# The low part of a weight tile: a subtraction on VectorE, or a negated copy on ScalarE and a transfer that adds

## The chip, the core and the metric

The kernel runs on one core of a Trainium2 chip. The time is that of one execution on the device, in microseconds, the median of the runs shown. A core has TensorE for matrix products, VectorE and ScalarE for elementwise work, GpSimd, and 16 DMA engines that move data; SyncE (SP in the profile) and GpSimd (POOL) issue transfers here. All of them run side by side and wait for each other by semaphores. Each engine takes its own instructions strictly in the order of the program.

## What is computed

Two layers of a transformer on 256 latent tokens and 256 context tokens of width 1024, all in float32. Per layer: a gated feed-forward, a mixer, another gated feed-forward, each with a norm that is modulated by a conditioning vector. The mixer of layer 0 is neighbourhood attention beside a long convolution, that of layer 1 is retention. In the last layer only the latents go on after the mixer.

```python
def swiglu(h, w_in, w_out):
    a, b = jnp.split(h @ w_in, 2, axis=-1)
    return (jax.nn.silu(a) * b) @ w_out
...
        mod_l = (jax.nn.silu(c) @ w_mod[i] + b_mod[i]).reshape(b, N_MOD, 1, D_MODEL)
        x_lat = x_lat + 0.5 * mod_l[:, 2] * swiglu(modulate(x_lat, norm_gain[i, 0], mod_l[:, 0], mod_l[:, 1]),
                                                 ffn_a_in[i], ffn_a_out[i])
...
            o_l, o_c = na_hyena_mixer(h_l, h_c, even_in[e], even_out[e], ...)
            o_l, o_c = retention_mixer(h_l, h_c, ret_in[o], ret_out[o], ...)
```

## The kernel before, in words

Tokens lie along the free axis of a tile and features along its 128 partitions; lat and ctx share one tile of 512 columns. Each float32 product is made of three products in the faster type `fp32r`: a number is split into a high part, its rounding to fp32r, and a low part, what is left. `mm3` (L207 to L210) adds high times high, high weight times low activation, and low weight times high activation; the last of the three is the one that reads the low part of the weight, `wlo`.

Weights come as 336 tiles of 128 x 1024 (512 KB) or, for the feed-forward's second matrix, 128 x 1408 (704 KB), listed in `worder` in the order of use. A tile goes through these steps, each in four buffers:

- `w_dma` (L132): SP issues the load of a tile into one of four raw buffers, `raw`.
- `w_split` (L142): ScalarE copies `raw` into `whi`, which rounds it; VectorE subtracts `whi` from `raw` into `wlo`. Then `w_dma` loads the tile that is to take the same raw buffer.
- `w_get` (L172): hands a tile to TensorE. Ahead of it, it splits up to three more tiles. So the split of the tile after the next two stands in the program right before TensorE's work on the present one, and its `whi` and `wlo` buffers are those of the tile TensorE has just left.

Two rarer ways to split are `w_halves` (the first four tiles) and `w_paged` (seven tiles at the norms, into other buffers).

The modulation vectors are made beside this on VectorE: `mod_step` (L226) takes one 512 KB tile `wm` of the modulation weights, multiplies it with the conditioning vector and sums it (the reductions `junk`, L237), and `m_dma` loads another. Two such steps go with each pair of tiles in most feed-forwards, so SP's order there is raw, raw, wm, wm. There are two buffers for `wm`.

A feed-forward has two halves. In each, 11 pairs of tiles (`pi`) give a gate and a value, which ScalarE and VectorE turn into the activation `sg` and its parts `ghi` and `glo`; then 8 tiles of 704 KB (`po`) add to the residual. On both streams a weight tile feeds 512 columns; in the last feed-forward and from the retention's output on only 256. The order of the work is that of the program (`manual_schedule`); nothing is reordered.

Of the kernel before, what the change touches and what calls it, by code (L numbers as in the profile page):

```python
# [30 lines left out]
# columns of the packed per-partition constants  # L31
# [18 lines left out]
def _mod_tiles():  # L50
    """(layer, index, feature block) of the modulation VectorE makes, in order."""
    return [(l, i, b) for l, i in [(0, j) for j in range(2, 9)] + [(1, j) for j in range(9)] for b in range(KB)]


def body(ctx, tc, I, out):
# [38 lines left out]
    # ---------------------------------------------------------------- constants  # L94
# [11 lines left out]
    # ---------------------------------------------------------------- weights  # L106
# [35 lines left out]
    def w_split():  # L142
        i = wpos["split"]
        if i >= len(worder):
            return
        while wpos["dma"] <= i:
            w_dma()
        n = worder[i][1]
        t = raws.pop(i)
        hi = whl.tile([P, WSLOT], F32R, tag="hi", name="whi")  # L150
        lo = whl.tile([P, WSLOT], F32R, tag="lo", name="wlo")
        act(hi[:, :n], t[:, :n], AF.Copy)
        V.tensor_tensor(out=lo[:, :n], in0=t[:, :n], in1=f(hi[:, :n]), op=ALU.subtract)  # L153
        hls[i] = (hi, lo)
        wpos["split"] += 1
        if not hold[0]:
            w_dma()

    def w_halves():
        """The next tile's split in two steps; nothing is loaded in its place."""  # L160
# [22 lines left out]
    def w_paged():  # L183
        """The next tile, split into pages: for where whl's buffers are all in use."""
# [27 lines left out]
    # ---------------------------------------------------------------- modulation  # L212
# [37 lines left out]
    # ---------------------------------------------------------------- residual and norms  # L250
# [8 lines left out]
    def sumsq(s, m, late=None):  # L259
        """Adds block m's squares; the addition itself is left to the caller where a list is given."""  # L260
# [16 lines left out]
    def rsqrt_steps(y, src, scale, n):  # L277
        """y (SBUF) = (src*scale + eps)^-1/2, src in PSUM; one VectorE operation between yields."""
# [25 lines left out]
    def norm_h(s, k, l, n, dst):  # L304
        """dst: (hi, lo) APs of block k, stream s. Returns what is left to do once hi is there."""
# [25 lines left out]
    # H: list of KB (hi, lo), each [P, 512] = lat | ctx  # L331
# [15 lines left out]
    class Norm:  # L347
        """Norm n of layer l, whose sums of squares are complete per stream in turn."""
# [29 lines left out]
    # ---------------------------------------------------------------- generic matrix products  # L378
    def out_gemm(acts, nk, tiles_per_m, l, n, lat_only, norm, late_acts=None):
        """X += gate * (W^T acts); acts: list of (hi, lo) [P, 512] or [P, 256]."""  # L380
# [85 lines left out]
    def first_group(norm, mid=None):  # L466
        """The first 4 feature tiles after a norm; the latents go first, the context's norm runs beside."""
# [39 lines left out]
    def scaled(norm, k):  # L507
        """Block k of the latents times the gain, not yet normed, for the products that run ahead of the norm.
        Two more columns hold the shift."""
# [14 lines left out]
    def first_group_lat(norm):  # L524
        """The first 4 feature tiles of a norm of the latents alone. They run ahead of the norm, whose factor
        of each row and whose shift's product the evacuation adds."""
# [43 lines left out]
    # ---------------------------------------------------------------- SwiGLU  # L570
# [52 lines left out]
    # ---------------------------------------------------------------- start  # L623
    FILT = {}

    def dft_load(j):
        """Table j of the transforms in two parts."""
# [5 lines left out]
    def parted(a, j):  # L633
        """a[j] becomes its two parts."""
# [79 lines left out]
    def decay_scalars():  # L714
        """Decay exponents: log_sigmoid of the logits."""
# [20 lines left out]
    def start():  # L736
# [78 lines left out]
        def normed(s, m):  # L815
            """Blocks 2m and 2m+1 of stream s, normed."""
# [93 lines left out]
    # ---------------------------------------------------------------- layer 0 mixer  # L910
    def mixer0(norm_in, norm_out):
# [62 lines left out]
        # attention  # L974
# [9 lines left out]
        def qk_split(b):  # L984
            """Queries and keys of heads 2b and 2b + 1 in two parts each."""
# [89 lines left out]
        def attend(i):  # L1075
            """One step of the attention: head i's scores, head i-1's transposes, head i-2's values."""
# [17 lines left out]
        # queries and keys  # L1094
# [19 lines left out]
        # values  # L1114
# [17 lines left out]
        # hyena projections, with the attention beside them  # L1132
# [93 lines left out]
    # ---------------------------------------------------------------- layer 1 mixer  # L1226
    def mixer1(norm_in, norm_out):
# [74 lines left out]
        def qk_parts(h):  # L1302
            """Queries and keys of head h in two parts each."""
            parted(kT[h], 0)
            parted(kT[h], 1)
            parted(qT, h)
# [119 lines left out]
def _layout(inp):  # L1426
# [4 lines left out]
    def featT(x):  # (256, 1024) -> (4, 128, 2*256)  # L1431
# [5 lines left out]
    def pcol(v):  # (..., n*128) -> (128, ...*n)  # L1437
# [29 lines left out]
    # first shift and scale: chunks of 2 feature blocks of each, per block of 128 inputs  # L1467
# [3 lines left out]
    def feat_tiles(w, n):  # (n*128? K, C) -> (C/128, 128, K/128*128)  # L1471
# [13 lines left out]
    def tok_tiles(w):  # (1024, C) -> chunks of 256 columns, halves of K: (C/256*2, 128, 4*256)  # L1485
# [22 lines left out]
    ph = 2 * np.pi * np.outer(np.arange(L), np.arange(L) + 0.5) / 512  # [t, k]  # L1508
# [5 lines left out]
    # relative position bias laid out per (query, key); keys outside the window hold a constant  # L1514
# [36 lines left out]
```

## Time and profile before

| | |
|---|---|
| Time, median of 3 runs | 1912.69 us (1911.32 to 1914.88) |
| Profiled execution, first to last instruction | 1918.3 us |
| TensorE busy | 1894.8 us, 99% |
| VectorE busy | 1210.1 us, 63% |
| of it subtractions for `wlo` (L153), 325 | 421.8 us |
| ScalarE busy | 701.5 us, 37% |
| GpSimd busy | 65.6 us, 3% |
| moved by SP's transfers | 273.76 MB |
| moved by GpSimd's transfers | 2.10 MB |

For the profiled execution the page gives its span and no other time; the span is 5.6 us over the median of the runs.

How to read it: an engine's busy time is the time its instructions ran, not the time it was needed. TensorE's matmuls overlap and their ends are modelled, so its pace is better read from the count in a stretch than from one matmul's length. A line can be that of a helper: all ScalarE copies stand at L89, so the tile's name tells them apart. "A <- B" in the list of waits says that A was held up by B, with total, times and longest. A stretch (a:b) is a piece of the span in microseconds; its row has the busy time and the count of each engine, then the granted TensorE clock, the mean busy share of the 16 DMA engines and the GB/s that they moved.

### The profile page before, as it was taken

The numbers are of one execution on the slowest core, as the hardware profiler recorded it, in microseconds if no ns is written. First come the engines' busy times: TensorE is split into PE (matmuls) and PEld (weight loads), VectorE is DVE, ScalarE is ACT, GpSimd is POOL, SyncE is SP. The second block draws the span as 40 slices with busy tenths as digits, with TensorE's granted clock in tenths as the row PEclk, the third lists the DMA queues.
The fourth block names the chain that finished last, engine by engine and source line by source line (L and its number), as shares of the span: only waits on it lengthen the run. The fifth ranks groups of instructions, "written<-read, shape, count | busy, mean of one in ns | idle before, by whom it ended". The sixth has DMA issues, their size and how long they took to land.

```text
span 1918.3 us, 26355 instructions
## 1 busy us (share of the span) xinstructions
PE 1894.8 (99%) x10646; PEld 1627.5 (85%) x10646; DVE 1210.1 (63%) x1870; ACT 701.5 (37%) x1085; POOL 65.6 (3%) x73
## 2 busy tenths in 40 slices
PE   8999999999999999999999999999999999999999
PEld 5788888798877798878887988888889999999999
DVE  5577677777676776676766655433346755567554
ACT  4332122245554352222222422122233544465442
POOL 1010000002001200000000000000000200000000
PEclk9999999999999999999999999999999999999999
DMA  9355445532323235554555256423323432355653
GB/s 355 117 175 197 150 165 183 200 95 82 99 66 92 77 108 166 174 197 144 185 193 169 85 190 209 142 88 94 116 82 99 133 100 88 100 178 184 197 181 129
DMA packets 77899, 277.52 MB, mean 145 GB/s; under 512 B 8657, under 2 KB 9681, under 8 KB 77650
## 3 DMA queue, kind: packets, MB, share of 16 engines
q1 hardware_dynamic: 76626, 273.76, 43.2%
q0 software_dynamic: 1152, 2.10, 0.4%
q8 instruction: 83, 1.36, 0.3%
q14 instruction: 38, 0.31, 0.0%
HBM read 274.77 MB, written 1.05 MB: 144 GB/s over the span
## 4 chain that ended last, share of the span: by engine, by line
PE 87%; DMA 5%; DVE 5%; issue 1%; ACT 1%; SPq 0%; POOL 0%; DVEq 0%; POOLq 0%; ACTq 0%
PE pi L208 13%; PE pi L209 13%; PE pi L210 13%; PE po L209 9%; PE po L208 9%; PE po L210 9%; DMA wm<-in_wmt_dram 5%; DVE wlo L153 2%; PE fg L208 2%; PE fg L210 2%; PE fg L209 2%; PE pv L1297 2%; PE pv L1296 2%; PE pv L1295 2%; DVE junk L237 1%
## 5 line engine op out<-in xcount | busy, mean ns | idle before, releaser
L208 PE MATMUL pi<-hhi,whi 128*128 128x512 f32 (+1 forms) x1488 | 545.9, 367 | 0.0
L210 PE MATMUL pi<-hhi,wlo 128*128 128x512 f32 (+1 forms) x1488 | 545.2, 366 | 0.0
L209 PE MATMUL pi<-hlo,whi 128*128 128x512 f32 (+1 forms) x1488 | 545.2, 366 | 0.0
L153 DVE TENSOR_TENSOR wlo<-raw,whi 128x1024 fp32r<-128x1024 f32 (+1 forms) x325 | 421.8, 1314 | 165.5 <-ACT whi L89 164.9
L89 ACT ACTIVATE whi<-raw 128x1024 fp32r<-128x1024 f32 (+1 forms) x329 | 363.9, 1115 | 394.0 <-PE po L209 161.5
L237 DVE CUSTOM_DVE_ANT_0 junk<-wm,scb,cst 128x1024 bf16<-128x1024 f32 x224 | 291.1, 1299 | 97.0 <-DMA wm<-in_wmt_dram 93.2
L208 PEld LDWEIGHTS pi<-hhi,whi 128*128 128x128 f32 x1488 | 279.8, 188 | 52.2 <-issue 1.1
L210 PEld LDWEIGHTS pi<-hhi,wlo 128*128 128x128 f32 x1488 | 279.6, 188 | 49.5
L209 PEld LDWEIGHTS pi<-hlo,whi 128*128 128x128 f32 x1488 | 279.6, 188 | 49.2
L208 PE MATMUL po<-ghi,whi 128*128 128x512 f32 (+1 forms) x770 | 271.1, 352 | 6.9 <-ACT ghi L89 6.9
L209 PE MATMUL po<-glo,whi 128*128 128x512 f32 (+1 forms) x770 | 270.2, 351 | 0.2 <-DVE glo L181 0.2
L210 PE MATMUL po<-ghi,wlo 128*128 128x512 f32 (+1 forms) x770 | 270.1, 351 | 0.0
L89 ACT ACTIVATE ghi<-sg 128x512 fp32r<-128x512 f32 (+1 forms) x88 | 50.9, 579 | 396.7 <-DVE sg L580 393.5
L208 PEld LDWEIGHTS po<-ghi,whi 128*128 128x128 f32 x770 | 145.7, 189 | 29.1 <-ACT ghi L89 8.2
L209 PEld LDWEIGHTS po<-glo,whi 128*128 128x128 f32 x770 | 145.8, 189 | 22.4 <-DVE glo L181 1.5
L210 PEld LDWEIGHTS po<-ghi,wlo 128*128 128x128 f32 x770 | 145.7, 189 | 20.4
L391 DVE SCALAR_TENSOR_TENSOR x<-po,gate,x 128x256 f32<-128x256 f32 x136 | 61.3, 480 | 126.2 <-PE po L210 125.9
L580 DVE TENSOR_TENSOR sg<-sg,pi 128x512 f32<-128x512 f32 (+1 forms) x79 | 49.1, 622 | 100.3 <-PE pi L210 99.1
L181 DVE TENSOR_TENSOR glo<-sg,ghi 128x512 fp32r<-128x512 f32 (+1 forms) x88 | 55.1, 626 | 56.9 <-ACT ghi L89 56.9
L89 ACT ACTIVATE sq<-x 128x256 f32<-128x256 f32 (+1 forms) x71 | 30.1, 439 | 120.3 <-DVE x L391 120.2
L1297 PE MATMUL pv<-whi,hlo 128*128 128x256 f32 x256 | 72.1, 282 | 0.0
L1295 PE MATMUL pv<-whi,hhi 128*128 128x256 f32 x256 | 72.1, 282 | 0.0
(331 smaller groups left out, 2438.7 us busy)
## 6 DMA issues: line engine op xcount, KB each, us to landing
raw<-in_ffi_dram SPq DMA_DIRECT2D x176, 512.0 KB, 3.7
wm<-in_wmt_dram SPq DMA_DIRECT2D x128, 512.0 KB, 4.5
raw<-in_ffo_dram SPq DMA_DIRECT2D x64, 704.0 KB, 4.8
raw<-in_rt_dram SPq DMA_DIRECT2D x64, 512.0 KB, 3.7
raw<-in_ev_dram SPq DMA_DIRECT2D x32, 512.0 KB, 3.6
wm<-in_wm_dram SPq DMA_DIRECT2D x32, 256.0 KB, 5.7
x<-in_xt_dram SPq DMA_DIRECT2D x8, 256.0 KB, 5.4
bias<-in_rpb_dram SPq DMA_DIRECT2D x8, 256.0 KB, 4.2
```

Source lines behind the costliest of these rows:

```text
L89: S.activation(out=out, in_=in_, func=func, **k)
L153: V.tensor_tensor(out=lo[:, :n], in0=t[:, :n], in1=f(hi[:, :n]), op=ALU.subtract)
L181: V.tensor_tensor(out=lo, in0=src, in1=f(hi), op=ALU.subtract)
L208: T.matmul(o, lhsT=w[0][:, c0:c1], rhs=x[0][:, x0:x1], start=start, stop=False)
L209: T.matmul(o, lhsT=w[0][:, c0:c1], rhs=x[1][:, x0:x1], start=False, stop=False)
L210: T.matmul(o, lhsT=w[1][:, c0:c1], rhs=x[0][:, x0:x1], start=False, stop=stop)
L237: V.tensor_tensor_reduce(out=junk, in0=t, in1=scb[:, s, :], scale=1.0, scalar=bcol, op0=ALU.mult, op1=ALU.add, accum_out=MOD[l][:, idx, b, ...
L391: V.scalar_tensor_tensor(out=xs(s, m), in0=p[:, c0:c0 + L], scalar=gate[:, m, s:s + 1], in1=xs(s, m), op0=ALU.mult, op1=ALU.add)
L580: V.tensor_tensor(out=sg, in0=sg, in1=pb[:, :w], op=ALU.mult)
L1295: T.matmul(po[tb], lhsT=H[k][0][:, hs_], rhs=w[0][:, ws_], start=k == 0, stop=False)
L1296: T.matmul(po[tb], lhsT=H[k][0][:, hs_], rhs=w[1][:, ws_], start=False, stop=False)
L1297: T.matmul(po[tb], lhsT=H[k][1][:, hs_], rhs=w[0][:, ws_], start=False, stop=k == KB - 1)
```

## The change

In `w_split` the low part is made in two steps. ScalarE writes minus the high part into `wlo`. Then a transfer that GpSimd issues reads `raw` and adds it onto what stands in `wlo`, so that `wlo` holds raw minus high as before. `w_halves`, `w_paged` and `split_to` keep VectorE's subtraction. The rest of the difference is comments taken out.

```diff
@@ w_split
         act(hi[:, :n], t[:, :n], AF.Copy)
-        V.tensor_tensor(out=lo[:, :n], in0=t[:, :n], in1=f(hi[:, :n]), op=ALU.subtract)
+        act(lo[:, :n], f(hi[:, :n]), AF.Copy, scale=-1.0)
+        G.dma_start(out=lo[:, :n], in_=t[:, :n], accum_op=ALU.add)
         hls[i] = (hi, lo)
```

Three places show how the instructions move. In all of them a name ends in a buffer number, "waits" lists what the instruction's engine waits for, DMAHW is a transfer of SP and DMASW one of GpSimd, and the line numbers of the changed kernel are one higher. The first is ScalarE in the last feed-forward, before and with the change, two pairs of tiles:

```order
L89 ACTIVATE whi_15914<-raw_15780 128x1024 [waits DMAHW1_49,PE_49,Activation_49]
L89 ACTIVATE whi_15945<-raw_15811 128x1024 [waits DMAHW2_49,PE_49,Activation_49]
L89 ACTIVATE sg_15976<-pi_15920 128x256 [waits PE_49]
L89 ACTIVATE ghi_15979<-sg_15976 128x256 [waits DVE_49]
L89 ACTIVATE whi_15983<-raw_15849 128x1024 [waits DMAHW3_49,PE_49,Activation_49]
```

```order
L89 ACTIVATE whi_15942<-raw_15805 128x1024 [waits DMAHW1_49,PE_49]
L89 ACTIVATE wlo_15943<-whi_15942 128x1024 [waits DMASW4_49,PE_49,Activation_49]
L89 ACTIVATE whi_15974<-raw_15837 128x1024 [waits DMAHW2_49,PE_49]
L89 ACTIVATE wlo_15975<-whi_15974 128x1024 [waits DMASW5_49,PE_49,Activation_49]
L89 ACTIVATE sg_16006<-pi_15949 128x256
L89 ACTIVATE ghi_16009<-sg_16006 128x256 [waits DVE_49]
```

Between a pair's activations there are four copies of a whole tile where there were two, and the added ones wait for TensorE to leave the buffer and for the transfer that added into it four tiles earlier.

The second is SP, whose raw loads in the same stage stood as the first fence shows and stand as the second does:

```order
L138 DMA raw_14502<-in_ffi_dram 128x1024 [waits DMAHW1_49,DVE_49]
L138 DMA raw_14527<-in_ffi_dram 128x1024 [waits DMAHW2_49,DVE_49]
L138 DMA raw_14540<-in_ffi_dram 128x1024 [waits DMAHW3_49,DVE_49]
L138 DMA raw_14553<-in_ffi_dram 128x1024 [waits DMAHW4_49,DVE_49]
L138 DMA raw_14566<-in_ffi_dram 128x1024 [waits DMAHW5_49,DVE_49]
```

```order
L138 DMA raw_14775<-in_ffi_dram 128x1024 [waits DMAHW1_49,DMASW0_49,Activation_49]
L138 DMA raw_14801<-in_ffi_dram 128x1024 [waits DMAHW2_49,DMASW1_49,Activation_49]
L138 DMA raw_14815<-in_ffi_dram 128x1024 [waits DMAHW3_49,DMASW2_49,Activation_49]
L138 DMA raw_14829<-in_ffi_dram 128x1024 [waits DMAHW4_49,DMASW3_49,Activation_49]
L138 DMA raw_14843<-in_ffi_dram 128x1024 [waits DMAHW5_49,DMASW4_49,Activation_49]
```

The order is the same; the raw buffer is now released by GpSimd's transfer and no longer by VectorE.

The third is GpSimd with the change, in the same stage; before, its queue is empty there:

```order
L154 DMA wlo_15604<-raw_15440 128x1024 [waits DMAHW0_49,DMASW3_49,Activation_49]
L154 DMA wlo_15646<-raw_15482 128x1024 [waits DMAHW1_49,DMASW4_49,Activation_49]
L154 DMA wlo_15688<-raw_15524 128x1024 [waits DMAHW2_49,DMASW5_49,Activation_49]
L154 DMA wlo_15730<-raw_15566 128x1024 [waits DMAHW3_49,DMASW6_49,Activation_49]
L154 DMA wlo_15762<-raw_15608 128x1024 [waits DMAHW4_49,DMASW7_49,Activation_49]
```

Each waits for ScalarE's negated copy.

## The prediction

> **What bounds the kernel now.** I read the page's busy shares first, then who made TensorE wait, then the chain of waits, then the transfers.
>
> ```profile
> span 1918.3 us, 26355 instructions
> PE 1894.8 (99%) x10646; PEld 1627.5 (85%) x10646; DVE 1210.1 (63%) x1870; ACT 701.5 (37%) x1085; POOL 65.6 (3%) x73
> q1 hardware_dynamic: 76626, 273.76, 43.2%
> q0 software_dynamic: 1152, 2.10, 0.4%
> ```
>
> TensorE is busy for 1894.8 of 1918.3 us. Nothing that makes another engine lighter can win more than the 23.5 us that are left. The transfers hold the 16 DMA engines for 43.2% of the span, 828.7 us for 273.76 MB, so a megabyte costs 3.03 us and a 512 KB tile (0.524 MB) 1.59 us of all 16 engines. That is the resource with the second largest claim, once it is read stage by stage.
>
> ```profile
> PE po L208 <- ACT ghi L89: 6.9, 3, 3.0
> PE pf L647 <- DMA cst<-in_cst_dram: 4.4, 1, 4.4
> SPq L138 <- DVE wlo L153: 1381.5, 305, 24.0
> ```
>
> Of TensorE's idle time 4.4 us is the wait for the first constants. The largest item that VectorE can be blamed for is 6.9 us: three times an output product waits for an activation tile `ghi` whose input comes late from VectorE. The last row shows what the load queue lives on: SP stands before a raw load until VectorE's subtraction has released the raw buffer, 305 times. The chain shows what makes VectorE late at those three places:
>
> ```profile
> 273.33 2.29 DVE wlo L153 x2
> 276.02 6.48 DMA wm<-in_wmt_dram
> 282.63 1.28 DVE junk L237
> 284.13 1.04 issue
> 285.25 2.28 DVE wlo L153 x2
> ```
>
> From one pair of subtractions to the next is 11.9 us: the subtractions release the raw buffers, SP issues the raw loads and then the modulation load behind them, that lands 6.48 us later, and its reductions keep VectorE from the next pair. TensorE needs less for the same pair of tiles: 48 matmuls at 52.00/225 us (the stretch 208 to 260 below), 11.1 us. VectorE falls behind by 0.8 us a pair until TensorE notices. This is a real cost of the subtraction, and it is small.
>
> **The change, part by part.** Removed: 325 subtractions on VectorE. Added: as many copies with a factor of -1 on ScalarE, and as many transfers issued by GpSimd that read the raw tile and the negated tile and write the sum.
>
> ```profile
> L153 DVE TENSOR_TENSOR wlo<-raw,whi 128x1024 fp32r<-128x1024 f32 x261 | 318.7, 1238 | 138.7 <-ACT whi L89 138.2
> L153 DVE TENSOR_TENSOR wlo<-raw,whi 128x1408 fp32r<-128x1408 f32 x64 | 103.4, 1623 | 26.7 <-ACT whi L89 26.7
> L89 ACT ACTIVATE whi<-raw 128x1024 fp32r<-128x1024 f32 x265 | 276.5, 1053 | 290.3 <-issue 122.9 <-PE po L209 89.2 <-PE pi L209 30.2
> L89 ACT ACTIVATE whi<-raw 128x1408 fp32r<-128x1408 f32 x64 | 87.6, 1374 | 103.8 <-PE po L209 72.3 <-issue 28.2 <-ACT whi L89 3.3
> ```
>
> VectorE loses 318.7 + 103.4 = 422 us and is worth at most the 6.9 us above, because elsewhere TensorE does not wait for it. I count 0 for the gain: the modulation loop keeps its transfer and gets a longer wait ahead of it (below), so the lag need not go.
>
> ScalarE gains 261 x 1.053 + 64 x 1.374 = 363 us, by the row of the same copy: 701.5 becomes 1064 us, 55%. Over the whole span TensorE covers this. In the last stage it nearly fills ScalarE:
>
> ```profile
> 1829.69 1.06 ACT L89 ACTIVATE whi<-raw 128x1024 fp32r<-128x1024 f32 x1 [0.87 <-ACT whi L89]
> 1830.65 0.37 ACT L89 ACTIVATE sg<-pi 128x256 f32<-128x256 f32 x1
> 1833.47 0.42 ACT L89 ACTIVATE ghi<-sg 128x256 fp32r<-128x256 f32 x1 [2.46 <-DVE sg L580]
> 1833.80 1.04 ACT L89 ACTIVATE whi<-raw 128x1024 fp32r<-128x1024 f32 x1
> ```
>
> A pair of tiles there has four copies of 1.05 us now, and 0.37 + 0.42 us: 5.0 us, against 2 x 24 matmuls at 175.00/1476 us (stretch 1690 to 1865 below), 5.7 us. ScalarE still fits, so 0. Without that cover it would cost the pair what goes over 5.7 us.
>
> The transfers are the heavy part. 261 tiles of 0.524 MB and 64 of 0.721 MB are 183 MB, two thirds of what the kernel moves now. No row shows a transfer that adds, so its price per byte is bounded in units of a load's 1.59 us per 512 KB. From below: its bytes need not come from the chip's main memory, so a little under one load, 0.7, can't be excluded. From above: two reads and one write, one after the other, each at a load's full price, make 3. A load reads once and writes once; this reads twice and writes once. If reading sets the pace it costs 2, if the total does 1.5. I take 2 (3.18 us a tile), since the only software-issued transfers in the trace, 0.4% of the span or 7.7 us for 2.10 MB, at 3.65 us a megabyte, lean dear rather than cheap.
>
> The Trainium skill's page "Collectives: The Full Stack" (section on the bandwidth ceiling) says that a reducing transfer is slower not by its addition but because it reads two sources through one read ring; it states a ratio of 1.93 to a plain copy. By that figure my price would be 3.07 us instead of 3.18 us, an estimate; no run here shows it yet.
>
> Where does it fit? Per stretch of the trace I add to the DMA share that is there the new demand: the subtraction's busy time in the stretch over 1.226 us (its median for a 512 KB tile) times 3.18 us, a factor of 2.6. What goes over the stretch's length is time. The first row has that median; then come the stretches, with DMA share and GB/s at the end of a row, and below them the subtraction alone in the same ones:
>
> ```profile
> L153 DVE TENSOR_TENSOR wlo<-raw,whi x325: 1205/1226/2310, 58.3 to 1900.7; 128x1024 fp32r<-128x1024 f32 x131, 128x1408 fp32r<-128x1408 f32 x32
> 156.00:208.00 52.00, 52.00 (x226) 41.98 (x225) 40.16 (x57) 11.47 (x11) 0.00 (x0) 1.00 0.57 191
> 208.00:260.00 52.00, 52.00 (x225) 42.03 (x224) 33.46 (x50) 11.59 (x14) 0.00 (x0) 1.00 0.43 145
> 260.00:362.00 102.00, 100.29 (x433) 80.87 (x431) 74.26 (x101) 25.94 (x33) 0.00 (x0) 1.00 0.53 181
> 783.00:1063.00 280.00, 275.38 (x1216) 223.22 (x1215) 192.97 (x275) 72.40 (x89) 0.00 (x0) 0.99 0.53 177
> 1170.00:1215.00 45.00, 45.00 (x196) 36.34 (x195) 26.22 (x34) 11.89 (x12) 0.00 (x0) 1.00 0.62 210
> 1690.00:1865.00 175.00, 174.88 (x1476) 174.82 (x1477) 114.90 (x165) 89.97 (x140) 0.00 (x0) 1.00 0.59 190
> 1865.00:1918.00 53.00, 49.99 (x422) 49.78 (x421) 24.90 (x28) 16.37 (x19) 0.00 (x0) 1.00 0.43 139
> ...
> 156.00:208.00 52.00, 14.02 (x9) 1.00 0.57 191
> 260.00:362.00 102.00, 22.41 (x18) 1.00 0.53 181
> 783.00:1063.00 280.00, 60.18 (x45) 0.99 0.53 177
> 1170.00:1215.00 45.00, 10.86 (x7) 1.00 0.62 210
> 1690.00:1865.00 175.00, 73.51 (x60) 1.00 0.59 190
> 1865.00:1918.00 53.00, 17.77 (x12) 1.00 0.43 139
> ```
>
> The stretch 1690 to 1865 is the last feed-forward on the latents alone, where a weight tile feeds half as many columns: 0.59 x 175 = 103 us of transfers, plus 73.51 x 2.6 = 191 us, make 294 us in 175: 119 over. The others, in order: 14.0, 10.2, 24.5, 11.1 and, for the last, 15.9. Sum 194.6 us. The stretches left out have room at this price; the longest, 1215 to 1690, keeps 44 us of it.
>
> Three waits are added. GpSimd's issue waits for ScalarE's second copy; behind it in GpSimd's queue stand only the other transfers and some 12 small subtractions, which wait for ScalarE anyway. SP's raw load waits for the adding transfer instead of the subtraction; behind it stand the modulation loads, and behind these the reductions. TensorE's third product waits for the transfer. Between stages these waits are covered by three tiles of matmuls; at the very start they are not:
>
> ```profile
> 57.24 2.01 ACT L89 ACTIVATE whi<-raw 128x1024 fp32r<-128x1024 f32 x2 [2.86 <-PE fg L209]
> 58.33 2.36 DVE L153 TENSOR_TENSOR wlo<-raw,whi 128x1024 fp32r<-128x1024 f32 x2 [3.48 <-ACT whi L89]
> 25.02 0.54 POOL L630 DMA_DIRECT2D dfthi<-in_dft_dram  x1
> dfthi<-in_dft_dram POOLq DMA_DIRECT2D x4, 256.0 KB, 5.3
> raw<-in_ffi_dram SPq DMA_DIRECT2D x176, 512.0 KB, 3.7
> ```
>
> The first split of the steady loop ends at 59.6 and TensorE takes it at once. Now the copy ends at 59.4, the issue takes 0.54, and landing takes 3.7 us by a raw load's row to about 6 by GpSimd's own loads: 4 to 7 us late, once; I take 6.
>
> A raw buffer's round in the narrow stage is then a load of 3.7 us, two copies of 1.06, an issue of 0.54, the addition with about 6, and SP: 12.4 us for four tiles, 3.1 us each. That is over TensorE's 2.85 us a tile but under the 4.8 us that load and addition hold the DMA engines, 1.59 + 3.18, so the engines decide and not the round.
>
> Sum: 194.6 + 6 = 201 us on the profiled span of 1918.3. That span is 5.6 us above the median of the runs shown, 1912.69, and I take the difference as it is: **2113 us**.
>
> **The rivals.**
>
> Cheap addition: the price is about one load. The same table at 1.59 us leaves only the last feed-forward over, by 23.6 us; with the start, 1942 us. For it: half of the reading is on the chip. Against it: twice the bytes read.
>
> Dear addition: three loads or more. The table gives 600 us at three; 2519 us. Then nearly all stretches are bound by transfers. For it: the additions are done row by row in engines whose arithmetic no row shows. Against it: nothing in the trace.
>
> The other side: VectorE's loop of 11.9 us against 11.1 was the lag, it goes with the subtraction, and the transfers fit. This gives back the 6.9 us and costs 4.2 us at the start with the quick landing, so 1910 us, or 1906 if the first copies come early enough. It decides only where an addition costs under 0.85 of a load, since in the narrow stage two plain loads, 3.18 us, already exceed a tile's 2.85 us. The Trainium skill's page "DMA: Bandwidth & Descriptors" (section on the anatomy of one DMA) would put it here: its fit of 2.0 us plus bytes over 436 GB/s makes 3.2 us for 512 KB, 1.2 us of it moving, an estimate of 0.76 of a load. But that fit is for copies.
>
> **How the numbers follow.** Price 1.5 to 2.4 loads (2003 to 2245 us by the same table): 0.56, the forecast. About one load, 1925 to 2003: 0.16. Dearer than 2.4: 0.19. No loss: 0.09, of which 0.04 is faster by over 0.2% and 0.05 within it (0.2% is about what a measurement of this kernel can tell from no change). Slower is 0.91. The forecast's own range is 2003 to 2245; 1940 to 2480 (a price of 2.9) leaves out the no-loss cases and half of the dear ones, together 2 in 10.
>
> **What would show it.** Right: the DMA share rises to nine tenths and more in the last three slices; TensorE waits for GpSimd's transfers at the third product there and hardly elsewhere but in the modulation stretches; the software queue of the page shows 183 MB more at about 6 us a megabyte, some 1110 us of its share. Wrong: if the share stays under 0.9 while TensorE waits, latency and not throughput is the limit; if slices in the middle, 362 to 783 and 1215 to 1690, stretch, the price is above 2.4.

## The result, and the profile after

The changed kernel takes 2119.18 us, the median of 4 runs (2108.07 to 2127.23), against 1913.79 us (1911.32 to 1916.76, 4 runs) for the kernel before: 1.1077 times as long, 95% interval 1.1038 to 1.1116. The forecast was 2113 us with a range of 1940 to 2480. The total is right to 6 us. The parts of the sum are not, and the experiments below show in the main why they made up for each other.

First the page of the changed kernel: span, busy times, and the two queues (packets, MB, share of the 16 DMA engines).

```profile
span 2125.4 us, 27260 instructions
PE 1959.3 (92%) x10646; PEld 1669.6 (79%) x10646; DVE 798.4 (38%) x1545; ACT 1061.4 (50%) x1410; POOL 338.3 (16%) x398
q0 software_dynamic: 47952, 185.09, 46.4%
q1 hardware_dynamic: 76626, 273.76, 37.5%
```

VectorE lost 412 us of work, ScalarE gained 360, and the span grew by 207.1 us. GpSimd's queue holds the 16 engines for 46.4% of 2125.4 us, 986 us for 185.09 MB: 5.33 us a megabyte, 2.80 us for a 512 KB tile. A load costs 37.5%, 2.91 us a megabyte, 1.53 us a tile. An adding transfer is thus worth 1.83 of this kernel's loads, or 1.76 of the loads before.

Next the list of waits, the load queue's and TensorE's (total, times, longest):

```profile
SPq L138 <- DMA wlo<-raw: 1680.5, 318, 27.4
...
PE pi L211 <- DMA wlo<-raw: 66.0, 43, 4.4
...
PE po L211 <- DMA wlo<-raw: 42.7, 22, 6.1
...
PE fg L211 <- DMA wlo<-raw: 21.6, 6, 5.3
...
PE po L209 <- ACT ghi L89: 17.7, 5, 7.1
```

L211 is the third product, the one that reads the low part. TensorE waits there for GpSimd's transfer, as the prediction said, but the row of `fg` is at norms, where it said that three tiles of matmuls cover the wait. Then the transfers' landing (KB each, median us from issue to landing):

```profile
wlo<-raw POOLq DMA_DIRECT2D x261, 512.0 KB, 6.5
raw<-in_ffi_dram SPq DMA_DIRECT2D x176, 512.0 KB, 5.6
wm<-in_wmt_dram SPq DMA_DIRECT2D x128, 512.0 KB, 7.7
```

A raw load of the feed-forward took 3.7 us before. The stretches of the changed kernel that hold the same matmuls as those of the prediction (busy time of each engine, then the granted clock, DMA share, GB/s):

```profile
162.30:218.30 56.00, 53.98 (x226) 42.95 (x225) 25.91 (x44) 21.13 (x18) 6.42 (x8) 0.97 1.01 272
...
381.50:819.40 437.90, 420.38 (x2286) 352.77 (x2287) 231.15 (x469) 237.31 (x413) 73.26 (x75) 0.97 0.65 167
819.40:1126.90 307.50, 283.34 (x1215) 227.79 (x1214) 141.80 (x240) 126.80 (x138) 38.75 (x45) 0.97 0.93 247
...
1292.50:1785.50 493.00, 478.37 (x2962) 427.78 (x2960) 145.27 (x302) 270.27 (x341) 87.91 (x97) 1.00 0.83 198
1785.50:2044.60 259.10, 202.65 (x1476) 194.31 (x1477) 42.43 (x105) 150.54 (x194) 47.73 (x56) 0.92 0.99 245
2044.60:2125.00 80.40, 58.44 (x422) 56.81 (x420) 7.26 (x16) 32.45 (x32) 11.19 (x13) 0.89 0.86 211
```

With every stretch cut at the same matmuls in both traces, the 207.1 us lie here. The last two columns belong to an experiment below, the change with the modulation loads issued one step earlier.

| stretch of before | long before | forecast | after | measured | reordered loads | over before |
|---|---|---|---|---|---|---|
| 0–54 | 54.0 | 0 | 53.9 | −0.1 | 51.8 | −2.2 |
| 54–156 | 102.2 | +6 | 108.3 | +6.1 | 108.8 | +6.6 |
| 156–208 | 52.0 | +14.0 | 56.0 | +4.0 | 52.0 | 0.0 |
| 208–260 | 51.8 | 0 | 51.8 | 0.0 | 51.8 | 0.0 |
| 260–362 | 102.8 | +10.2 | 111.4 | +8.6 | 100.1 | −2.7 |
| 362–783 | 420.3 | 0 | 437.9 | +17.6 | 429.0 | +8.7 |
| 783–1063 | 279.9 | +24.5 | 307.5 | +27.6 | 272.7 | −7.2 |
| 1063–1170 | 107.1 | 0 | 115.2 | +8.1 | 112.7 | +5.6 |
| 1170–1215 | 45.1 | +11.1 | 50.4 | +5.3 | 45.1 | 0.0 |
| 1215–1690 | 474.9 | 0 | 493.1 | +18.2 | 494.8 | +19.9 |
| 1690–1865 | 174.9 | +118.9 | 259.1 | +84.2 | 254.1 | +79.2 |
| 1865 to the last matmul | 50.2 | +15.9 | 77.7 | +27.5 | 70.3 | +20.1 |

So there are three groups: the last feed-forward (the last two rows) with +111.7 us where 134.8 were forecast; the four stretches with modulation that the table charged, +45.5 for 59.8; and all the others, +49.9, where only the 6 us of the start were (they stand at 59.6 in the prediction, so in 54–156). These are the numbers of one trace each: in that of a variant below, with the change ahead of tile 260 alone, the same four stretches are 60.8 us longer and not 45.5. What is called the last feed-forward here, as in the prediction, begins with the rest of the retention's output, which also feeds 256 columns; that ends at 1726.7 in the kernel before.

### The profile page after: what moved, and what is told of

It is laid out like the page before. It is cut to its first block, busy times and chain, and to the rows that moved or that the text cites. A ratio compares the mean times of both kernels' runs of the same rounds, so it can differ in the third digit from the quotient of the medians.

```text
span 2125.4 us, 27260 instructions
## 1 busy us (share of the span) xinstructions
PE 1959.3 (92%) x10646; PEld 1669.6 (79%) x10646; DVE 798.4 (38%) x1545; ACT 1061.4 (50%) x1410; POOL 338.3 (16%) x398
## 3 DMA queue, kind: packets, MB, share of 16 engines
q0 software_dynamic: 47952, 185.09, 46.4%
q1 hardware_dynamic: 76626, 273.76, 37.5%
## 4 chain that ended last, share of the span: by engine, by line
PE 36%; issue 32%; DMA 22%; DVE 3%; POOL 3%; ACT 3%; POOLq 0%; SPq 0%; ACTq 0%; DVEq 0%
DMA wlo<-raw 11%; PE pi L209 5%; PE pi L211 5%; PE pi L210 5%; DMA raw<-in_ffo_dram 3%; DMA raw<-in_ffi_dram 3%; DMA wm<-in_wmt_dram 3%; POOL wlo L154 3%; PE po L211 2%; PE po L209 2%; PE po L210 2%; ACT whi L89 1%; DMA raw<-in_rt_dram 1%; PE pv L1297 1%; PE pv L1298 1%
## 5 line engine op out<-in xcount | busy, mean ns | idle before, releaser
L211 PE MATMUL pi<-hhi,wlo 128*128 128x512 f32 (+1 forms) x1488 | 558.4, 375 | 66.1 <-DMA wlo<-raw 66.0
L209 PE MATMUL pi<-hhi,whi 128*128 128x512 f32 (+1 forms) x1488 | 554.3, 373 | 0.0
L210 PE MATMUL pi<-hlo,whi 128*128 128x512 f32 (+1 forms) x1488 | 552.8, 372 | 0.0
L154 POOL DMA_DIRECT2D wlo<-raw x325 | 280.5, 863 | 1686.3 <-ACT wlo L89 1412.0
L211 PEld LDWEIGHTS pi<-hhi,wlo 128*128 128x128 f32 x1488 | 286.6, 193 | 128.3 <-DMA wlo<-raw 78.4
L89 ACT ACTIVATE wlo<-whi 128x1024 fp32r<-128x1024 f32 (+1 forms) x325 | 365.0, 1123 | 10.3
L210 PEld LDWEIGHTS pi<-hlo,whi 128*128 128x128 f32 x1488 | 286.8, 193 | 49.9
L211 PE MATMUL po<-ghi,wlo 128*128 128x512 f32 (+1 forms) x770 | 277.2, 360 | 24.9 <-DMA wlo<-raw 24.8
L211 PEld LDWEIGHTS po<-ghi,wlo 128*128 128x128 f32 x770 | 151.1, 196 | 48.2 <-DMA wlo<-raw 27.9
L211 PE MATMUL fg<-hhi,wlo 128*128 128x256 f32 (+1 forms) x200 | 63.0, 315 | 15.8 <-DMA wlo<-raw 15.8
L182 DVE TENSOR_TENSOR glo<-sg,ghi 128x512 fp32r<-128x512 f32 (+1 forms) x88 | 55.1, 626 | 56.9 <-ACT ghi L89 56.9
L1297 PE MATMUL pv<-wlo,hhi 128*128 128x256 f32 x256 | 71.9, 281 | 1.3 <-DMA wlo<-raw 1.3
```

Of the source, the lines that this page charges most:

```text
L89: S.activation(out=out, in_=in_, func=func, **k)
L154: G.dma_start(out=lo[:, :n], in_=t[:, :n], accum_op=ALU.add)
L182: V.tensor_tensor(out=lo, in0=src, in1=f(hi), op=ALU.subtract)
L209: T.matmul(o, lhsT=w[0][:, c0:c1], rhs=x[0][:, x0:x1], start=start, stop=False)
L210: T.matmul(o, lhsT=w[0][:, c0:c1], rhs=x[1][:, x0:x1], start=False, stop=False)
L211: T.matmul(o, lhsT=w[1][:, c0:c1], rhs=x[0][:, x0:x1], start=False, stop=stop)
```

## The experiments

The theory was that of the prediction: transfers bind the last feed-forward and the modulation stretches by throughput. The rivals are ScalarE's longer queue, the landing of the low part in front of the third product, and rounds of waits between SP, GpSimd, VectorE and ScalarE. Each time stands beside the kernel before on the same chip (medians 1913.89 to 1914.33 us).

**The price of adding: a copying transfer.** The same transfer, without the addition.

```diff
-        G.dma_start(out=lo[:, :n], in_=t[:, :n], accum_op=ALU.add)
+        G.dma_start(out=lo[:, :n], in_=t[:, :n])
```

> As the changed kernel, but GpSimd's transfer copies the raw tile over the low part instead of adding it, so the low part holds the raw tile and the result is not the reference's. Same number, size, issue and waits; one read less per byte. Theory (engine time of the two reads sets the loss): the price falls from 2.80 us per 512 KB tile (46.4% of 2125.4 us for 185.09 MB) to about a load's 1.5 to 1.6, so by the table of the prediction some 25 us in the narrow stage and some 20 to 40 us at stage edges: 1950 to 1980 us. Rival (the length of the chain of a tile, not the engines' time): landing falls only from 6.5 to about 5 us and most of the loss stays, over 2040 us.

Measured: 1970.24 us, ratio 1.0285 (1.0256 to 1.0314). Its software queue:

```profile
q0 software_dynamic: 47952, 185.09, 26.3%
```

The span there is 1959.5 us, so the same 185.09 MB take 515 us of the engines, 2.78 us a megabyte. Adding costs 5.33 / 2.78 = 1.92 times as much, and the 512 KB tile lands after 4.2 us instead of 6.5. Adding instead of copying is worth 149 us of the kernel; no run here tells the second read from the addition itself. The Trainium skill's page "Collectives: The Full Stack" (section on the bandwidth ceiling) states 1.93 for a reducing transfer against a copying one, measured between cores; the runs here agree, for a transfer inside one core's own memory.

**ScalarE alone.** The negated copy stays; VectorE adds in place of the transfer.

```diff
         act(lo[:, :n], f(hi[:, :n]), AF.Copy, scale=-1.0)
-        G.dma_start(out=lo[:, :n], in_=t[:, :n], accum_op=ALU.add)
+        V.tensor_tensor(out=lo[:, :n], in0=t[:, :n], in1=f(lo[:, :n]), op=ALU.add)
```

> ScalarE writes the negated high part as in the changed kernel, but VectorE adds the raw tile onto it; no adding transfer. Theory (the transfers cost the time): 1914 us as before, at most 10 us more for the longer chain of a tile. Rival (ScalarE's 325 added copies, 363 us, hold up its queue): most of the 205 us stays, 2050 us or more.

Measured: 1956.35 us, ratio 1.0225 (1.0204 to 1.0246), 42 us over the kernel before: a miss. The loss is in the last feed-forward, whose two stretches went from 174.9 to 202.4 and from 50.2 to 56.9 us. ScalarE's timeline there (start, duration, instruction, what it waited for):

```profile
1886.21 0.42 ACT L89 ACTIVATE ghi<-sg 128x256 fp32r<-128x256 f32 x1 [1.36 <-DVE sg L581]
1886.54 1.04 ACT L89 ACTIVATE whi<-raw 128x1024 fp32r<-128x1024 f32 x1
1887.61 1.06 ACT L89 ACTIVATE wlo<-whi 128x1024 fp32r<-128x1024 f32 x1
1888.58 1.05 ACT L89 ACTIVATE whi<-raw 128x1024 fp32r<-128x1024 f32 x1
1889.66 1.06 ACT L89 ACTIVATE wlo<-whi 128x1024 fp32r<-128x1024 f32 x1
1890.62 0.37 ACT L89 ACTIVATE sg<-pi 128x256 f32<-128x256 f32 x1
1892.34 0.42 ACT L89 ACTIVATE ghi<-sg 128x256 fp32r<-128x256 f32 x1 [1.35 <-DVE sg L581]
```

From one `ghi` to the next are 6.13 us; TensorE's pair takes 5.7. The 5.0 us of work that the prediction counted are there, but ScalarE takes its instructions in order and idles 1.36 us between `sg` and `ghi`, until VectorE has multiplied. Counting the work left out the gap. But 0.43 us in each of 22 pairs is under 10 of the 34.2 us that the two stretches lost; the rest was not taken apart. In this variant VectorE's addition also stands behind the copy, so the 42 us are an upper bound for the copies.

**The transfer alone, as a copy.** Neither negated copy nor addition.

```diff
-        act(lo[:, :n], f(hi[:, :n]), AF.Copy, scale=-1.0)
-        G.dma_start(out=lo[:, :n], in_=t[:, :n], accum_op=ALU.add)
+        G.dma_start(out=lo[:, :n], in_=t[:, :n])
```

> GpSimd's transfer copies the raw tile into the low part's place and ScalarE writes no negated part, so its two copies per pair in the narrow stage are as before the change; the low part holds the whole raw tile instead of the remainder. The variant with a copying transfer and the negated copy took 1970, the variant with the negated copy and no transfer 1956. If what is left there of the loss is ScalarE's queue in the narrow stage, this one loses it: 1915 to 1935 us, and the stretch of 174.9 us is at most 185. If it is the transfer itself (two loads' worth per tile, 103 + 88 = 191 us of the DMA engines in 174.9), it stays at 1950 to 1970 us.

Measured: 1924.60 us, ratio 1.0058 (1.0036 to 1.0080). The two stretches are 189.3 and 54.3 us long. The total is what the theory of ScalarE's queue expected, the first stretch is 4 us above its limit. So of the copying variant's loss in the last feed-forward (+37.1 us) half needs ScalarE's copies; alone they gave +34.2, the copying transfer alone +18.5. They overlap, they do not add.

**The adding transfer alone, from tile 262 on.** That is the retention's output from its third tile and the last feed-forward. Nobody reads the sum, and of 704 KB tiles only 512 KB are moved. Two waits are added all the same: ScalarE's next copy into the same buffer of the high part waits until the transfer has read it, and GpSimd's transfer waits for the one before the last, which adds into the same half of the table.

```diff
         V.tensor_tensor(out=lo[:, :n], in0=t[:, :n], in1=f(hi[:, :n]), op=ALU.subtract)
+        if i >= 262:
+            c = i % 2 * D
+            G.dma_start(out=scb.rearrange("p a b -> p (a b)")[:, c:c + D], in_=f(hi[:, :D]), accum_op=ALU.add)
```

> VectorE's subtraction stays in every tile. From the last feed-forward on (tiles 262 to 335) GpSimd issues besides, per tile, an adding transfer of 512 KB whose source is the high part and whose destination is a table that nobody reads any more; no engine waits for its result but the next writer of that high part. So ScalarE has no added copy, SP and TensorE no added wait: only the load on the 16 DMA engines is added. Theory (the DMA engines' throughput makes the narrow stage long): at 2.80 us per added 512 KB, as the changed kernel's software queue shows, the stretch of 174.9 us needs 103 + 60 x 2.80 = 271 us, so +96, and the tail 23 + 12 x 2.80 = 57 for 50, so +6: about 2015 us, 1985 to 2030, with a DMA share of 0.9 and more there. Rival (ScalarE's longer queue and the landing of the low part make it long, the engines only look busy): under +40, at most 1955 us.

Measured: 1987.54 us, ratio 1.0386 (1.0361 to 1.0412). Its stretches with the matmuls of the last feed-forward, then the two added waits in the whole run:

```profile
1680.90:1910.90 230.00, 198.82 (x1476) 188.16 (x1477) 109.77 (x159) 88.55 (x134) 46.88 (x54) 0.95 1.03 264
1910.90:1981.60 70.70, 57.63 (x422) 55.70 (x420) 27.32 (x32) 20.61 (x24) 13.93 (x16) 0.88 0.98 240
```

```profile
POOL scb L156 <- DMA scb<-whi: 186.9, 56, 6.2
...
ACT whi L89 <- DMA scb<-whi: 104.8, 48, 4.1
```

The DMA share is 1.03 and 0.98 and the stretches are 55.1 and 20.4 us longer, without a copy more on ScalarE. That is 75.5 of the change's 111.7 us, and the 16 tiles of 704 KB there would add 0.197 MB each, 16 x 0.197 x 5.33 = 17 us of the engines: an estimate of 92 us. So the transfers by themselves, with no wait of TensorE for their sum, carry most of the loss. That this is throughput and not the two added waits is argued from their own time: in the first stretch the software queue has 65.5% of the 230 us for 28.56 MB and the load queue 37.2%, together 236 us of transfers where TensorE needs 174.9. The price is no effect of the crowd: 5.27 us a megabyte here, and 5.41 in 1292.5–1785.5 of the changed kernel, at a share of 0.83 (50.8% of 493 us for 46.29 MB). No run has the transfers without any added wait, and what the remaining 20 us are, queue or landing, no run here separates.

**The two halves of the change.** Once only from tile 260 on (the retention's output and the last feed-forward), once only ahead of it, with `i < 260` in the condition.

```diff
+        if i >= 260:
             act(lo[:, :n], f(hi[:, :n]), AF.Copy, scale=-1.0)
             G.dma_start(out=lo[:, :n], in_=t[:, :n], accum_op=ALU.add)
+        else:
+            V.tensor_tensor(out=lo[:, :n], in0=t[:, :n], in1=f(hi[:, :n]), op=ALU.subtract)
```

> The change for the last 76 tiles alone (the retention's output product and the last feed-forward, which feed 256 columns); all tiles before them are split by VectorE. Theory (the narrow stage loses by itself, 84 and 27 us in the two stretches of the changed trace): 2015 to 2035 us. Rival (the narrow stage was late from what came before it): under 1980 us.

> The change only in tiles 0 to 259, that is everywhere but in the last feed-forward. The mirror of the kernel that had it only there and took 2021, 107 us over before. If the two halves of the loss add up, this one takes 2119 - 107 = 2012 us (2000 to 2020). My table of stretches gave 14.0 + 10.2 + 24.5 + 11.1 + 6 at the start = 66 us for this part at two loads, and 15 to 25 at the 1.75 loads that the changed kernel's queue showed: 1930 to 1940 us if only throughput and the start count there. So about 2012 says that some 75 us come from something the table leaves out.

Measured: 2021.18 us, ratio 1.0573 (1.0535 to 1.0611), and 2018.64 us, ratio 1.0549 (1.0523 to 1.0575). The halves add: 107 + 104 = 211 us, against 205. The wide half is thus as dear as the narrow one, and the table gave it 66 us.

**The order of the modulation loads.** The changed kernel, with `m_dma` one tile ahead, so that a modulation load no longer stands behind the raw loads of its own pair.

```diff
-            while mpos["dma"] <= i:
+            while mpos["dma"] <= min(i + 1, len(mlist) - 1):
```

> The changed kernel with the modulation tiles' loads one step earlier in SP's order, as in the variant that took 1904. If a good part of the change's loss in the wide stages is SP's order (a modulation load behind raw loads that wait for an adding transfer, and VectorE late behind that), it takes 2070 to 2095 us. If the low part's landing before the third product makes that loss, the order of SP's loads does little: 2100 to 2125 us.

Measured: 2050.59 us, ratio 1.0718 (1.0694 to 1.0742), 69 us less than the change, beyond what either theory gave. Four of its stretches, with the same matmuls as 156–208, 260–362, 783–1063 and 1170–1215 of before:

```profile
160.60:212.60 52.00, 52.00 (x225) 42.07 (x224) 26.83 (x46) 21.33 (x18) 6.45 (x8) 1.00 1.04 295
264.40:364.50 100.10, 100.10 (x433) 81.14 (x432) 54.44 (x84) 48.46 (x53) 15.49 (x18) 1.00 1.03 287
793.60:1066.20 272.60, 272.60 (x1215) 222.47 (x1214) 136.97 (x228) 123.50 (x132) 37.03 (x43) 1.00 1.00 275
1179.00:1224.00 45.00, 45.00 (x195) 36.43 (x194) 13.19 (x22) 21.23 (x19) 6.02 (x7) 1.00 1.03 305
```

In all four TensorE is busy without a gap, at the full clock, while the same tiles are added by the same transfers. The DMA share is 1.00 to 1.04, higher than in the change itself. So throughput did not cost time in these stretches: the share alone does not tell a stage that is bound by transfers from one that they just fill. What cost time is a round of waits. The timeline of the changed kernel without TensorE, inside 783–1063 of before:

```profile
856.03 5.26 SPq L138 DMA_DIRECT2D raw<-in_ffo_dram  x2
...
861.40 2.72 SPq L223 DMA_DIRECT2D wm<-in_wmt_dram  x2
...
873.10 1.28 DVE L238 CUSTOM_DVE_ANT_0 junk<-wm,scb,cst 128x1024 bf16<-128x1024 f32 x1 [13.29 <-DMA wm<-in_wmt_dram]
...
875.64 0.68 DVE L581 TENSOR_TENSOR sg<-sg,pi 128x512 f32<-128x512 f32 x1
...
876.36 0.63 ACT L89 ACTIVATE ghi<-sg 128x512 fp32r<-128x512 f32 x1 [15.26 <-DVE sg L581]
...
878.29 1.38 ACT L89 ACTIVATE wlo<-whi 128x1408 fp32r<-128x1408 f32 x1
...
879.96 0.86 POOL L154 DMA_DIRECT2D wlo<-raw  x1 [17.49 <-ACT wlo L89]
```

SP issues the modulation loads behind raw loads that wait for adding transfers; VectorE's reductions wait 13.29 us for the tile; `sg`, the activation's product, stands behind them on VectorE; ScalarE waits 15.26 us for `sg` before `ghi`, and the next tile's copies stand behind `ghi`; GpSimd's transfer waits 17.49 us for those. TensorE has a gap of 7.12 us at 877.0. The subtraction left VectorE, and VectorE is in the round still, by way of ScalarE's queue.

**The round without TensorE's wait.** VectorE subtracts as before; GpSimd then adds the high part onto the raw tile, a sum that is not read.

```diff
         V.tensor_tensor(out=lo[:, :n], in0=t[:, :n], in1=f(hi[:, :n]), op=ALU.subtract)
+        if i < 260:
+            G.dma_start(out=t[:, :n], in_=f(hi[:, :n]), accum_op=ALU.add)
```

> VectorE's subtraction stays everywhere. In tiles 0 to 259 GpSimd adds the high part onto the raw tile once the subtraction has read it, a sum that nobody reads. So the transfers and their bytes are those of the change in these tiles, the raw buffer is released by the transfer as in the change (a little later even), but TensorE's third product no longer waits for a transfer, and ScalarE has no added copy. If the loss of these stages (some 98 us) is the landing of the low part in front of the third product, with the half-clock stretches that these stalls draw behind them, most of it goes: 1915 to 1940 us. If it is the DMA engines' throughput or the raw buffers' slower round, it stays: 1990 to 2020 us.

Measured: 2238.65 us, ratio 1.1694 (1.1675 to 1.1713). Both theories missed, by more than 200 us. TensorE waits for no adding transfer at all, so the landing in front of the third product is not needed for a loss; and in the stretch shown throughput is not either. VectorE's subtraction is still in this round and no longer in that of the change, so the run shows that such a round costs time, and not how much the change's own costs. Its timeline without TensorE, and one of its stretches:

```profile
378.32 2.36 DVE L153 TENSOR_TENSOR wlo<-raw,whi 128x1024 fp32r<-128x1024 f32 x2
379.83 0.86 POOL L155 DMA_DIRECT2D raw<-whi  x1 [15.62 <-DVE wlo L153]
...
384.45 3.14 SPq L138 DMA_DIRECT2D raw<-in_ffi_dram  x2
...
387.68 0.86 SPq L224 DMA_DIRECT2D wm<-in_wmt_dram  x2
393.06 1.28 DVE L239 CUSTOM_DVE_ANT_0 junk<-wm,scb,cst 128x1024 bf16<-128x1024 f32 x1 [7.86 <-DMA wm<-in_wmt_dram]
...
395.59 2.36 DVE L153 TENSOR_TENSOR wlo<-raw,whi 128x1024 fp32r<-128x1024 f32 x2
```

```profile
345.00:415.00 70.00, 52.24 (x193) 40.79 (x194) 34.87 (x49) 12.04 (x16) 7.08 (x9) 0.87 0.68 180
```

From pair to pair are 17.3 us, at a DMA share of 0.68. It is the round of 11.9 us that the prediction read from the chain of before, with one link more: the adding transfer, from 379.83 until SP goes on at 384.45. TensorE's pair needs 11.1 us.

**What a stall costs.** The kernel before with 11 pauses, in each of which TensorE waits for a small load.

```diff
+    def pause():
+        o = pso.tile([16, 16], F32, tag="po", name="pgap")
+        T.matmul(o, lhsT=gap, rhs=gap, start=True, stop=True)
+        G.dma_start(out=gap, in_=I["dft"][0, 0][:, :16])
+        o = pso.tile([16, 16], F32, tag="po", name="pgap")
+        T.matmul(o, lhsT=gap, rhs=gap, start=True, stop=True)
```

> The kernel before, with 11 pauses in the second half of a feed-forward on both streams: TensorE runs a matmul of 16 x 16, GpSimd loads 8 KB over its operand, and TensorE waits for that before it goes on. Nothing else waits longer. If a stall costs only its own length (some 2.5 to 3 us each), the kernel takes about 30 us more, 1940 to 1946 us. If each stall is followed by a stretch in which TensorE is granted half its clock, as behind the stalls in the trace of the changed kernel (3.4 or 6.8 us long, so 1.7 to 3.4 us lost), it takes 50 to 65 us more, 1962 to 1980 us, and the profile shows some 11 more such stretches.

Measured: 1953.97 us, ratio 1.0215 (1.0193 to 1.0237), between the two. TensorE's gaps are 2.26 to 2.46 us, 25.5 us in all, shorter than expected. The stage's row, and below it one of the kernel before in the same feed-forward (the clock is the third number from the end):

```profile
1210.00:1420.00 210.00, 184.46 (x734) 145.03 (x734) 56.69 (x65) 41.24 (x49) 5.92 (x11) 0.89 0.26 80
```

```profile
1215.00:1397.50 182.50, 182.50 (x787) 147.41 (x786) 67.44 (x78) 46.87 (x56) 0.00 (x0) 1.00 0.31 101
```

Of the 734 matmuls 44 belong to the pauses. The other 690 would take 160.0 us at the pace of the second row; they took 210.0, 4.5 us more for each pause, and elsewhere this trace is some 10 us shorter than that of before. Beside the gaps 24.5 us remain, 2.2 a pause, and most of them come with the clock: the trace has a stretch at half clock at each of the 11 pauses, nine of 3.4 and two of 6.8 us, 44.4 us in all. Half of that, 22 us, is what a TensorE that never waits would lose in them, an estimate.

The Trainium skill's page "TensorE: Matmul & The Clock Gate" (Part 1) has the clock halved after an idle window of about 3.4 us, counted on a free-running clock. The stretches' lengths agree; but here gaps of 2.3 us were enough, 11 times of 11, and the measurement decides. The length of a gap alone does not tell: behind one of 3.09 us in the changed kernel, which ends at 1073.23, the granted clock stays at 1.00 (1070 to 1086).

**What relieving VectorE is worth.** Three ways: no low part at all (the third product reads the high part), the modulation loads one step ahead in the kernel before (the edit shown above), and GpSimd subtracting every second tile in the stages with modulation.

```diff
-        V.tensor_tensor(out=lo[:, :n], in0=t[:, :n], in1=f(hi[:, :n]), op=ALU.subtract)
-        hls[i] = (hi, lo)
+        hls[i] = (hi, hi)
```

```diff
+        if i % 2 and (i < 60 or 92 <= i < 180):
+            G.tensor_tensor(out=lo[:, :n], in0=t[:, :n], in1=f(hi[:, :n]), op=ALU.subtract)
+        else:
             V.tensor_tensor(out=lo[:, :n], in0=t[:, :n], in1=f(hi[:, :n]), op=ALU.subtract)
```

> The low part of the 325 weight tiles is not made at all, by nobody; the third product reads the high part instead, so the result is not the reference's. It bounds what any relief of VectorE could win. Theory (VectorE holds TensorE up at three places only, 6.9 us, and the clock falls after them): 8 to 14 us less than before, 1900 to 1906 us. Rival (VectorE's 422 us cost TensorE more than the waits show): below 1890 us.

> The kernel before, VectorE's subtraction and all, with the modulation tiles' loads one step earlier in SP's order, so that a load no longer stands behind the raw loads of the same pair. My prediction held that VectorE falls behind TensorE since raw load, modulation load and reductions follow one another, 11.9 us a pair against TensorE's 11.1, and that this lag is worth up to 6.9 us. Leaving the low part out altogether gave 13.3 us. If the modulation load's place in SP's order makes the lag: 1900 to 1908 us. If VectorE's own work does (the subtraction of 2.3 us a pair and the reductions), or nothing that matters: 1911 to 1915, no change.

> Another way to take subtractions off VectorE: in the stages with modulation, GpSimd makes the low part of every second tile (i odd, below 60 and from 92 to 179) by a subtraction of its own, 74 tiles; VectorE keeps the rest. No transfer and no copy is added. GpSimd's subtraction of 512 columns takes 1.3 to 2.2 us in the trace of before, so 2.6 to 4.4 us for a tile, against 11.1 us of TensorE for a pair: it fits. If VectorE's lag is what costs up to 13 us (the variant without low parts): 1901 to 1908 us. If GpSimd and VectorE hinder each other or GpSimd is late before the third product: 1914 us and more.

Measured: without the low part 1900.80 us, ratio 0.9934 (0.9916 to 0.9951), so the 422 us of subtractions were worth 13 us. With earlier modulation loads 1904.27 us, ratio 0.9952 (0.9937 to 0.9966): one line gets 10 of them and beats both kernels. With GpSimd's help 1906.44 us, ratio 0.9959 (0.9946 to 0.9972). The reductions' group, first of the kernel before, then with earlier loads (busy us, mean ns, idle time ahead and its cause):

```profile
L237 DVE CUSTOM_DVE_ANT_0 junk<-wm,scb,cst 128x1024 bf16<-128x1024 f32 x224 | 291.1, 1299 | 97.0 <-DMA wm<-in_wmt_dram 93.2
```

```profile
L237 DVE CUSTOM_DVE_ANT_0 junk<-wm,scb,cst 128x1024 bf16<-128x1024 f32 x224 | 291.1, 1299 | 5.1
```

VectorE's 93.2 us of waiting for modulation tiles are gone, the work is the same. So the lag is that of the whole round: moving the load in SP's order ends it, and so does taking subtractions out of it, all of them or every second.

## Why the prediction was right, point by point

**The price.** It was taken as 2 loads, 3.18 us a tile; it measured 2.80 us, 1.76 loads, in the lower part of the forecast's 1.5 to 2.4. The argument from two reads fits: adding costs 1.92 times the copy, though no run tells the second read from the addition. The queue's share is 986 us where "some 1110" were named.

**The last feed-forward.** Forecast +134.8, measured +111.7. The mechanism is borne out by the transfer whose sum nobody reads, with the two waits named there. With the measured price the first stretch needs 103 + 73.51 x 2.80 / 1.226 = 271 us, against 259.1 measured and 294 forecast. The mis-sized term is the price.

**ScalarE.** "ScalarE still fits, so 0": this step failed. The copies alone cost up to 42 us, in part since the wait between `sg` and `ghi` belongs to the pair too: 6.13 us for TensorE's 5.7. Beside the adding transfer little of the failure can show, at most the 20 us left open above, because the pace there is 8.4 us a pair (259.1 us for 1476 matmuls, 48 to a pair). This is the first of the errors that happened to cost little.

**The modulation stretches.** The table's 59.8 us met 45.5 (60.8 in the other trace), but by another mechanism: the reordered loads take all of it away with the same transfers. At the measured price the table itself would give 26 us there. The step that failed is the reading that a demand over the stretch's length becomes time and that nothing else does. The prediction had the right round in its hands, 11.9 us against 11.1, and used it only as a possible gain; a longer link in it was a loss. For the narrow stage it did set up a round, and there "the engines decide and not the round" held.

**The start.** 6 us "once": the stall is 4.35 us, at 64.3, a stretch of 3.4 us at half clock follows, and 54–156 is 6.1 us longer. But such stalls come where other stages begin, too, and not once. The timeline's rows of the changed kernel at five of these places, where a norm or a projection begins (a sixth, 5.30 us at 1844.9, is at the norm of the last feed-forward):

```profile
456.30 0.58 PE L211 MATMUL fg<-hhi,wlo 128*128 128x256 f32 x1 [4.45 <-DMA wlo<-raw]
735.47 0.58 PE L211 MATMUL fg<-hhi,wlo 128*128 128x256 f32 x1 [3.76 <-DMA wlo<-raw]
1146.55 0.39 PE L211 MATMUL fg<-hhi,wlo 128*128 128x256 f32 x1 [3.81 <-DMA wlo<-raw]
1529.54 0.58 PE L211 MATMUL fg<-hhi,wlo 128*128 128x256 f32 x1 [3.74 <-DMA wlo<-raw]
1785.53 0.58 PE L211 MATMUL po<-rohi,wlo 128*128 128x256 f32 x1 [4.80 <-DMA wlo<-raw]
```

"Between stages these waits are covered by three tiles of matmuls" failed: the first and these five together are 24.9 us, and they stay when the loads are reordered.

**What the sum left out.** Many of the stalls are followed by half clock. The changed kernel spends 133.1 us of its span at half clock, the kernel before 23.9. Outside the last feed-forward that is 75.2 against 23.9, so some 26 us lost, an estimate (half of the difference). In the stretches that stood at 6 us in the forecast and measured +49.9, it is 41.0 against 20.0, some 10 us, and the five stalls at edges ahead of the last stage are 20.1 us: 30 of 50. The rest, small stalls in 362–783 and 1215–1690 and the 3.9 us by which the variant with the negated copy alone lengthens the latter, was not taken apart further.

**The gain.** Counted 0, "at most the 6.9 us". The bound was too low, 13 us: TensorE's waits aside, the kernel before spends 23.9 us at half clock and the one without low parts 6.8, half of which difference is 8.5 us. The change got none of it, since its longer round took the subtraction's place.

**The rivals.** The dear addition and the cheap one fell with the measured price. The other side needed under 0.85 of a load; even the copying transfer without ScalarE's copies is slower than before, at 1924.60 us. Of the signs named, the DMA share of nine tenths came true in the stretch that decides (0.99); of the page's last three slices two read nine tenths and the last one eight. That TensorE would wait hardly elsewhere did not come true, by the stalls at the edges. "If slices in the middle stretch, the price is above 2.4" was a wrong sign: 362–783 and 1215–1690 stretched by 17.6 and 18.2 us at a DMA share of 0.65 and 0.83, in good part because of the stage edges.

In sum, a price too high by 14% and a throughput term that was none stood against stalls at stage edges, half clock and a round that were missing. At the measured price the table and the start would have given some 2052 us, 67 under the time. That the errors nearly cancel is luck; the narrow stage, more than half of the loss, is not.

## What to carry to other kernels

When an operation is moved to a transfer, draw the whole round that its buffer goes through, every queue with what stands ahead in it, and compare its period with the consumer's, stage by stage; a table of busy shares sees neither rounds nor in-order gaps. Look first at the order of issues in a shared load queue: one line there was worth 10 us before the change and 69 us after it, while taking 422 us of work off an engine that seldom held TensorE up was worth 13. A DMA share near 1 is not yet a bound: it stood in stretches that lost nothing, so compare the transfers' own time in a stretch with what the consumer needs there.

## What the runs showed of the hardware that was not expected

Pauses of 2.3 us in a busy TensorE were each met by 3.4 or 6.8 us at half clock, so a pause cost 4.5 us instead of 2.3.

GpSimd's issue of an adding transfer took longer than that of the copy from the same tile. First the changed kernel, then the variant with a copy and no negated part:

```profile
L154 POOL DMA_DIRECT2D wlo<-raw x325 | 280.5, 863 | 1686.3 <-ACT wlo L89 1412.0
```

```profile
L153 POOL DMA_DIRECT2D wlo<-raw x325 | 172.7, 532 | 1558.7 <-PE pi L210 727.5
```

863 ns stand against 532. And a DMA share of 1.00 to 1.04 was compatible with a TensorE that never waited, over 272.6 us at a stretch.
